# Cached keys of the sample branch: 32x32 blocks turned by VectorE, scores as four row-tiled products

## The chip, the core and the metric

The kernel runs on one core of a Trainium2 chip. The metric is the device time of one execution in microseconds; the lower, the better. The kernel before takes 2191.76 us (median of three runs, 2189.55 to 2191.92).

A core has a matrix engine (TensorE, PE in the profile, with its weight loads shown apart as PEld), VectorE (DVE), ScalarE (ACT), GpSimd (POOL) and SyncE (SP), which here issues nearly all transfers. [...] Matrix products write to PSUM, of which there are eight banks of 128 partitions and 512 float32 columns.

## The reference

One inference step of one layer: a prompt of 256 tokens and 8 sample sequences of 8 new tokens each, that have 1024 cached tokens. All rows go through one input projection; two mixers (a gated delta rule and an attention over chosen keys) run on its columns, and the results are merged and projected again. The change concerns the second mixer for the sample sequences:

```python
def indexer_topk(qi, wi, kidx, q_pos, topk):
    logits = jnp.einsum('bqhd,bkd->bqhk', qi, kidx) * (IDX_DH ** -0.5)
    score = jnp.einsum('bqhk,bqh->bqk', jax.nn.relu(logits), wi) * (IDX_HEADS ** -0.5)
    score = jnp.where(causal[None], score, -jnp.inf)
    _, idx = lax.top_k(score, topk)
    return idx, idx <= q_pos[None, :, None]

def sparse_attention(q, k_sel, v_sel, valid):
    s = jnp.einsum('bqngd,bqknd->bqngk', qg, k_sel) * (ATT_DH ** -0.5)
    s = jnp.where(valid[:, :, None, None, :], s, -jnp.inf)
    p = jax.nn.softmax(s, axis=-1)
    return jnp.einsum('bqngk,bqknd->bqngd', p, v_sel)

# dsa_sample: kidx, k and v of the 1024 past tokens come from paged caches
# through page_table; the 8 new tokens of the sequence stand behind them
```

For each sample sequence the indexer has 16 heads x 8 tokens = 128 query rows of length 128 against 1024 cached index keys, and the attention has 16 heads in two groups with one key head each (n = 0, 1), so 2 x 64 query rows of length 128 against 2 x 1024 cached keys. 256 keys are kept per token.

## The kernel before, in words

**Main stream.** `stream` walks through 464 units. A unit is half of the 2048 rows of a 128-column block of a weight matrix. Its float32 weights are loaded (`raw`, six halves of 512 KB), split by ScalarE into a rounded high part (`whi`) and by VectorE into the rest (`wlo`), and 24 products with the 320 activation columns are made (`pm<-xh,whi`, `pm<-xl,whi`, `pm<-xh,wlo`). `split_ahead` splits two units ahead, with three buffers of each part. Units 0 to 119 are the attention columns and gates, unit 120 opens the delta-rule part.

**Side work.** Everything else is written as Python generators. `side_round` is called twice a unit, after 12 of the 24 products and at the end, and lets each generator emit its next piece if the planner's own clock (`Clock`) says that its operands are there. The order on every engine is so fixed when the program is built; the clock's costs only decide where a piece falls between the main products. All engines run that order; the real waits are semaphores.

**The sample branch** (`sample_branch`, L1337 and on) is one generator over the 8 sequences b, first for the indexer, then for the attention.

- A gather by GpSimd brings keys into a buffer of the `a8` ring (`a` in the profile): partition p holds 8 rows of the cache, each of 128 (indexer) or 2 x 128 numbers (attention).
- `tr4` turns a 128x128 piece by four TensorE transposes of 32 partitions each (`ps<-ident,a`, 32x32 results over four PSUM banks), and `out4` brings the four banks back by two ScalarE and two VectorE copies. An indexer sequence takes 8 pieces (32 transposes), an attention sequence 16 (64 transposes). The probabilities `pr` of the attention are turned in the same way; the change leaves that as it is.
- Indexer (L1369 to L1401): `ps<-a,qiS`, two products of 128x512 with the query as weights, and `ps<-kidxT,qiS` for new keys, float32 (two instructions to a product); ReLU by ScalarE; a product with head weights (`wsel`); the row goes to `scs` by a transfer.
- `scs` [64, 1088] goes through 32 rounds of `max` and `match_replace` on VectorE, and gives the mask `bs`.
- Attention (from L1440): for three column ranges the mask is laid into PSUM by a bf16 product (`ps<-bs,esel`), and the scores are added (`ps<-a,qS`, 64 output partitions for each n, and `ps<-kT,qS` for the new keys). Then a maximum, exponentials with sums, the turned probabilities, the product with V (`ps<-a,a`), and `sample_out`.

**Buffers.** Six PSUM banks (`ps`) serve all side work, two (`pm`) the main stream. Transfers are issued by SP in program order; an instruction at the head of its queue that waits holds those behind it.

## Time and profile before

| | before |
|---|---|
| median of 3 runs | 2191.76 us |
| the profiled execution | 2190.04 us |
| its span in the profile | 2188.3 us |
| busy: PE / PEld / DVE / ACT / POOL | 99% / 93% / 63% / 46% / 21% |
| granted TensorE clock | 0.998 |
| mean transfer rate | 198 GB/s |

In the profile a row of the timeline has the start, the duration, engine, line, operation, the names (out<-in, buffer numbers left out), shapes, type and a count. Matrix products are pipelined: a product's duration holds its way through the array, and the next one starts before it has ended, so costs are read from start to start. All instructions go through one helper and carry line 61; the tile names tell them apart.

### The profile page before, as it was taken

The page shows a single profiled execution, that of the slowest core. Times are in us where ns is not written, and L with a number is a line of the kernel's source. Part 1 is how long each engine was busy: PE and PEld are TensorE (multiplying, and loading weights), DVE is VectorE, ACT ScalarE, POOL GpSimd, SP SyncE. Part 2 cuts the span into 40 slices and gives each one's busy share as a digit, 9 for nine tenths or more (in the row PEclk, how much of TensorE's full clock was granted, in tenths as well). Part 3 has the DMA queues.
Part 4 walks back from the last instruction along what each step waited for, and adds up shares of the span by engine and source line. Part 5 has one row for each costly group of instructions (what it writes and reads, how often), then busy time and mean ns, then how long its engine had stood idle before and what let it go on. Part 6 is the DMA issues. An engine that isn't in the chain of part 4 may idle for free.

```text
span 2188.3 us, 43683 instructions
## 1 busy us (share of the span) xinstructions
PE 2157.9 (99%) x17151; PEld 2041.2 (93%) x17151; DVE 1384.4 (63%) x2807; ACT 1002.9 (46%) x2207; POOL 458.2 (21%) x624
## 2 busy tenths in 40 slices
PE   7999999999999999999999999999999999999997
PEld 6889988999888999899999999999999999999997
DVE  4665447789644477777777777777756545545543
ACT  3225464343343455474646464646445434233343
POOL 1000100000000008361717171717270000000000
PEclk9999999999999999999999999999999999999999
DMA  9985549765666667686768686867786966655562
GB/s 333 354 281 151 155 120 264 218 188 142 186 209 203 192 170 196 169 217 186 217 177 219 178 220 177 219 178 212 184 233 187 279 194 201 177 151 155 154 183 87
DMA packets 709839, 433.14 MB, mean 198 GB/s; under 512 B 67936, under 2 KB 697024, under 8 KB 707328
## 3 DMA queue, kind: packets, MB, share of 16 engines
q1 hardware_dynamic: 705536, 407.67, 66.1%
q0 software_dynamic: 3616, 21.02, 2.8%
q8 instruction: 135, 2.21, 0.4%
q10 hardware_dynamic: 480, 1.65, 0.2%
q14 instruction: 72, 0.59, 0.1%
HBM read 382.09 MB, written 47.89 MB: 196 GB/s over the span
## 4 chain that ended last, share of the span: by engine, by line
PE 67%; issue 23%; DVE 5%; DMA 3%; ACT 1%; SPq 0%; DVEq 0%; POOL 0%; POOLq 0%
PE pm L61 51%; PE ps L61 17%; DVE S L61 2%; DMA raw<-in_w_ada_dram 1%; DVE ps L61 1%; ACT ot L61 1%; DVE wlo L61 1%; DVE w L61 0%; DMA raw<-in_w_in_dram 0%; DMA cst<-in_conv_w_dram 0%; ACT vt L61 0%; SPq L61 0%; ACT whi L61 0%; DVE sc L61 0%; DMA c<-in_c_sample_dram 0%
## 5 line engine op out<-in xcount | busy, mean ns | idle before, releaser
L61 PE MATMUL pm<-xh,whi 128*128 128x320 f32 x3284 | 1004.4, 319 | 2.0 <-ACT whi L61 1.7
L61 PE MATMUL pm<-xl,whi 128*128 128x320 f32 x3284 | 971.6, 309 | 0.3 <-DVE xl L61 0.3
L61 DVE TENSOR_TENSOR wlo<-raw,whi 128x1024 fp32r<-128x1024 f32 x474 | 596.4, 1265 | 311.1 <-ACT whi L61 294.4
L61 PEld LDWEIGHTS pm<-xh,whi 128*128 128x128 f32 x3284 | 617.3, 188 | 34.3 <-issue 25.5
L61 PEld LDWEIGHTS pm<-xl,whi 128*128 128x128 f32 x3284 | 617.5, 188 | 1.5 <-DVE xl L61 0.8
L61 ACT ACTIVATE whi<-raw 128x1024 fp32r<-128x1024 f32 x474 | 497.9, 1058 | 158.7 <-PE pm L61 141.4
L61 PE MATMUL pm<-xh,wlo 128*128 128x320 f32 x3284 | 553.4, 309 | 0.0
L61 PEld LDWEIGHTS pm<-xh,wlo 128*128 128x128 f32 x3284 | 499.4, 188 | 0.0
L61 POOL TENSOR_TENSOR X<-X,tmpx 48x31 f32<-48x31 f32 (+15 forms) x248 | 184.0, 742 | 19.4
L61 POOL TENSOR_TENSOR tmpx<-blk,X 48x31 f32<-48x31 f32 (+15 forms) x248 | 156.4, 631 | 53.1 <-DMA blk<-d_b 21.7
L61 PE MATMUL pm<-y1h,whi 128*128 128x320 f32 x512 | 151.3, 309 | 1.1 <-ACT y1h L61 1.1
L61 PE MATMUL pm<-y1l,whi 128*128 128x320 f32 x512 | 151.2, 308 | 0.1
L61 DVE SCALAR_TENSOR_TENSOR ps<-xp,cs,ps 128x344 f32<-128x344 f32 x192 | 111.5, 581 | 6.8
L61 POOL TENSOR_TENSOR sc<-sc,mh 128x6 f32<-128x6 f32 (+1 forms) x24 | 43.6, 1815 | 328.6 <-DVE ct L61 136.6
L61 POOL TENSOR_TENSOR rfin<-rfin,mh 128x3 f32<-128x3 f32 x1 | 0.8, 848 | 486.7 <-DVE rfin L61 486.7
L61 PEld LDWEIGHTS pm<-y1h,whi 128*128 128x128 f32 x512 | 95.9, 187 | 1.3 <-ACT y1h L61 1.3
L61 PEld LDWEIGHTS pm<-y1l,whi 128*128 128x128 f32 x512 | 96.0, 187 | 0.3 <-DVE y1l L61 0.3
L61 PE MATMUL pm<-y1h,wlo 128*128 128x320 f32 x512 | 85.4, 308 | 0.0
L61 PEld LDWEIGHTS pm<-y1h,wlo 128*128 128x128 f32 x512 | 77.8, 187 | 0.0
L61 DVE SCALAR_TENSOR_TENSOR S<-S,gtr,ps 128x128 f32<-128x128 f32 x256 | 67.5, 344 | 0.1
L61 ACT ACTIVATE a<-ps 128x256 f32<-128x256 f32 (+3 forms) x96 | 50.1, 557 | 37.8 <-PE ps L61 36.6
L61 ACT ACTIVATE xp<-pm 128x256 f32<-128x256 f32 (+1 forms) x128 | 32.0, 303 | 69.7 <-PE pm L61 69.7
(360 smaller groups left out, 2317.5 us busy)
## 6 DMA issues: line engine op xcount, KB each, us to landing
raw<-in_w_in_dram SPq DMA_DIRECT2D x336, 512.0 KB
raw<-in_w_pa_dram SPq DMA_DIRECT2D x64, 512.0 KB
rawx<-in_w_ada_dram SPq DMA_DIRECT2D x18, 1024.0 KB
a<-in_w_ada_dram SPq DMA_DIRECT2D x16, 1024.0 KB
S<-in_state_gdn_dram SPq DMA_DIRECT2D x32, 512.0 KB
out_dram<-S SPq DMA_DIRECT2D x32, 512.0 KB
raw<-in_w_pb_dram SPq DMA_DIRECT2D x32, 512.0 KB
raw<-in_w_out_dram SPq DMA_DIRECT2D x32, 512.0 KB
```

The costliest lines, as they stand in the source:

```text
L61: made = fn(*args, **kw)
```

## The change

The stationary operand of the scores becomes a piece of the query that covers 32 of its 128 numbers, and the moving operand the 32 partitions of a block-turned key buffer.

1. `turn` replaces `tr4` and `out4` for keys: one VectorE transpose of 128x1024 in 32x32 blocks (per indexer sequence), two in place (per attention sequence). A turned block has the numbers of one 32-group j in its partitions, and there are four groups g of cache rows on the four partition groups.
2. The query must lie in all four partition groups. `spread` writes `qiS` (or `qS`) to a DRAM tensor in four transfers, in the layout [b, 32, 4, 128]; `fill` reads the piece of one sequence back four times, once per partition group, into half of the query's own buffer (`slot`, two sequences at a time). The next sequence but one is filled after the products of the present one.
3. The scores of an indexer sequence are 16 products (j, g) of 32 partitions, 128 weights and 256 columns, that add up over j in four banks (one per g). Those of an attention sequence are 32 products (j, g, n) of 32 partitions, 64 weights and 256 columns.
4. The new keys' scores are made for all sequences at once in `spread` (`newi`, `newk`) by products of 8 columns; VectorE adds `newk` later.
5. The mask is laid into five banks in place of three, with all 128 partitions as the contraction (`esel`, `bs` padded with zeros). There are five maxima and five exponentials in place of three each, four ReLU pieces in place of three; the orders of columns in `rl`, `sb`, `bs` and `pr` follow.
6. `Clock.cost` gets a factor for the new products.

```diff
-            part *= 0.62 if k <= 64 else 1.0
+            part *= 0.29 if k == 32 and rhs.shape[1] == NB else 0.62 if k <= 64 else 1.0
...
+        self.d_qi, self.d_q = (self.dram.tile([NB, 32, 4, 128], F32, name=n) for n in ("d_qi", "d_q"))
...
         if self.bq_n == 16:
-            self.flags.add("qS")
+            self.spawn(self.spread(self.qS, self.d_q, self.newk, [self.kT[:, n, :] for n in range(2)], 2, "qR"))
...
+    def fill(self, q, dram, b):
+        t = self.slot(q, b)
+        for j in range(4):
+            self.nc.sync.dma_start(t[32 * j:32 * j + 32], dram[b])
+
+    def spread(self, q, dram, new, keys, heads, flag, **kw):
+        yield self.ready(q, *keys)
+        yield from self.need(self.ps_side)
+        p = self.psum()
+        w = 128 // heads
+        for b in range(NB):
+            for n in range(heads):
+                s = slice(w * n, w * n + w)
+                self.mm(p[s, 8 * b:8 * b + 8], q[:, b, s], keys[n][:, NP + 8 * b:NP + 8 * b + 8], skip=True)
+        self.act(new, p[:, 0:64].rearrange("p (b t) -> p b t", t=TS), **kw)
+        self.ps_side.put(p)
+        for j in range(4):
+            self.nc.sync.dma_start(dram[:, :, j, :].rearrange("b r h -> r b h"), q[32 * j:32 * j + 32])
+        yield max(self.idle(q), self.ready(dram))
+        self.fill(q, dram, 0)
+        self.fill(q, dram, 1)
+        self.flags.add(flag)
...
-            for c0, c1 in self.SEGS:
-                yield from self.need(self.ps_side)
-                p = self.psum()
-                rhs = raws[b][:, 1024 + c0:1024 + c1] if c0 < NKEY else self.kidxT[:, NP:NT]
-                self.mm(p[:, 0:c1 - c0], self.qiS[:, b, :], rhs)
-                self.act(rl[:, c0:c1], p[:, 0:c1 - c0], AF.Relu, scale=SC)
-                self.ps_side.put(p)
+            yield from self.need(self.ps_side, 4)
+            ps = [self.psum() for _ in range(4)]
+            kt = raws[b][:, 1024:2048].rearrange("p (e j c) -> p j e c", e=8, j=4)
+            q = self.slot(self.qiS, b)
+            for j in range(4):
+                for g in range(4):
+                    r = slice(32 * g, 32 * g + 32)
+                    self.mm(ps[g][:, 0:256].rearrange("p (e c) -> p e c", e=8), q[r, j, :], kt[r, j],
+                            start=(j == 0), stop=(j == 3), skip=True)
...
+            if b + 2 < NB:
+                self.fill(self.qiS, self.d_qi, b + 2)
             if b + 1 < NB:
-                yield from keys_t(b + 1)
+                turn(raws[b + 1][:, 1024:2048], raws[b + 1][:, 0:1024])
...
-            for j in range(16):
-                self.tr4(ps, j, K[b][:, 128 * j:128 * j + 128])
-            self.out4(ps, 16, K[b])
+            for c in range(0, 2048, 1024):
+                turn(K[b][:, c:c + 1024], K[b][:, c:c + 1024])
...
+            for g, (p, w) in enumerate(zip(ps, width)):
+                self.mm(p[:, 0:w], es, self.bs[:, 256 * g:256 * g + w], start=True, stop=True)
+            for j in range(4):
+                for g in range(4):
+                    for n in range(2):
+                        r, s = slice(32 * g, 32 * g + 32), slice(64 * n, 64 * n + 64)
+                        self.mm(ps[g][s, 0:256].rearrange("r (e c) -> r e c", e=8), qr[r, j, s], ktv[r, n, j],
+                                start=False, stop=True, skip=True)
+            own = ps[4][:, 8 * b:8 * b + 8]
+            self.tt(own, own, self.newk[:, b, :], OP.add)
```

The order on TensorE in the indexer, at the second sequence, before; `pm` rows are the main stream, `a_1756` the keys of this sequence and `a_1757` those of the next.

```order
L61 MATMUL pm_65<-xl,whi_80 128x320
L61 MATMUL ps_68<-a_1756,qiS 128x512
L61 MATMUL ps_67<-a_1756,qiS 128x512
L61 MATMUL ps_70<-kidxT,qiS 128x64
...
L61 MATMUL pm_65<-xh,wlo_83 128x320 x8
L61 MATMUL ps_71<-ident,a_1757 128x32
...
L61 MATMUL ps_67<-a_1758,wsel 8x512 x2
L61 MATMUL ps_67<-a_1758,wsel 8x64
```

Three score products stand in one place, and half a unit later 32 transposes (of which one is shown) stand ahead of the product with the head weights. The same place after the change, with `a_1760` as the keys:

```order
L61 MATMUL pm_66<-xl,whi_79 128x320
L61 MATMUL ps_69<-a_1760,qiS 128x256
L61 MATMUL ps_67<-a_1760,qiS 128x256
L61 MATMUL ps_70<-a_1760,qiS 128x256
L61 MATMUL ps_71<-a_1760,qiS 128x256
...
L61 MATMUL pm_66<-xh,wlo_82 128x320 x8
L61 MATMUL ps_72<-a_1762,wsel 8x512 x2
L61 MATMUL ps_72<-newi,wsel 8x8
```

The four products stand there four times over (j = 0 to 3), the transposes are gone from TensorE, and 12 main products still stand between the scores and `wsel`.

The order on TensorE at the scores of the first attention sequence, before:

```order
L61 LDWEIGHTS esel
L61 MATMUL ps_67<-bs,esel 128x512
L61 MATMUL ps_67<-a_1755,qS 64x512 x2
L61 LDWEIGHTS esel
L61 MATMUL ps_71<-bs,esel 128x512
L61 MATMUL ps_71<-a_1755,qS 64x512 x2
L61 LDWEIGHTS esel
L61 MATMUL ps_69<-bs,esel 128x64
L61 MATMUL ps_69<-kT,qS 64x64 x2
```

Mask and scores alternate. After the change:

```order
L61 MATMUL ps_67<-bs,esel 128x256
L61 LDWEIGHTS esel
L61 MATMUL ps_69<-bs,esel 128x64
L61 MATMUL ps_71<-a_1759,qS 64x256 x2
L61 MATMUL ps_70<-a_1759,qS 64x256 x2
L61 MATMUL ps_72<-a_1759,qS 64x256 x2
L61 MATMUL ps_67<-a_1759,qS 64x256 x2
```

Five masks now come first (the last two are shown), then all products of the keys, eight for each j. The next use of the probabilities on TensorE (their transposes) stands 48 main products and the 64 key transposes later before, and 36 main products later after the change.

The order on VectorE behind the scores of the second attention sequence after the change:

```order
L61 TENSOR_TENSOR ps_67<-ps_67,newk 128x8
L61 TENSOR_REDUCE st_1766<-ps_67 128x1
L61 TENSOR_REDUCE st_1766<-ps_68 128x1
L61 TENSOR_REDUCE st_1766<-ps_71 128x1
L61 TENSOR_REDUCE st_1766<-ps_70 128x1
L61 TENSOR_REDUCE st_1766<-ps_72 128x1
L61 TENSOR_REDUCE st_1766<-st_1766 128x1 x2
L61 RECIPROCAL st_1766<-st_1766 128x1
L61 STREAM_TRANSPOSE a_1760<-a_1760 128x1024 x2
L61 TENSOR_TENSOR wlo_82<-raw_77,whi_79 128x1024
```

The two transposes of the next sequence's keys stand between the reciprocal and the next low part `wlo` of the main stream.

The order on SP in the middle of the indexer after the change:

```order
L61 DMA qiS<-d_qi 32x512 x4
L61 DMA scs<-a_1763 8x1088
L61 DMA raw_76<-in_w_in_dram 128x8x128 x2
L61 DMA qiS<-d_qi 32x512 x4
L61 DMA scs<-a_1763 8x1088
L61 DMA raw_77<-in_w_in_dram 128x8x128 x2
```

Before, a sequence had two loads `raw` and one `scs` there; four short reads of the query come to them.

## The prediction

> **What bounds the kernel now.** I read the page first, for the engines' shares, then the table of stretches for the two stages of the sample branch, and then the timeline of TensorE inside them. Timeline columns are start, duration, engine, line, operation, names, shape, count.

> ```profile
> span 2188.3 us, 43683 instructions
> PE 2157.9 (99%) x17151; PEld 2041.2 (93%) x17151; DVE 1384.4 (63%) x2807; ACT 1002.9 (46%) x2207; POOL 458.2 (21%) x624
> PE 67%; issue 23%; DVE 5%; DMA 3%; ACT 1%; SPq 0%; DVEq 0%; POOL 0%; POOLq 0%
> ```

> PE is busy nearly always, and the chain of waits that ended last (third row) runs mostly over PE. The stretches:

> ```profile
> 224.00:333.00 109.00, 109.00 (x892) 92.45 (x892) 46.84 (x94) 62.41 (x109) 7.47 (x8) 1.00 0.50 138
> 333.00:570.00 237.00, 237.00 (x1818) 226.20 (x1817) 195.13 (x318) 91.39 (x194) 3.98 (x7) 1.00 0.70 202
> 570.00:750.00 180.00, 180.00 (x1988) 152.95 (x1987) 81.24 (x146) 69.22 (x140) 15.30 (x26) 1.00 0.62 188
> ```

> The columns of the stretches are window, length, then busy PE, PEld, DVE, ACT, POOL, the granted clock, DMA share and GB/s. The indexer lies in the first stretch, the 32 selection rounds in the second, the attention in the third. PE is busy all the time in each, at clock 1.00, so it never waits there. A busy PE is not proof of a full one, so I go by start times: they show that the main products follow each other at a fixed rate, and that each piece of side work pushes all later ones back.

> ```profile
> 233.17 7.04 PE pm L61 x48
> ```

> This is 0.147 us a main product. The cost of a side piece is the start of the second main product behind it, less the start of the last one ahead of it, less 2 x 0.147 = 0.29. What the change takes from PE in these stages is time of the kernel; what it moves to VectorE or SP costs nothing until PE has to wait.

> **The indexer.** Before, a sequence costs PE these pieces:

> ```profile
> 262.51 0.31 PE L61 MATMUL pm<-xl,whi 128*128 128x320 f32 x1
> 262.66 1.88 PE L61 MATMUL ps<-a,qiS 128*128 128x512 f32 x4
> 264.37 0.33 PE L61 MATMUL ps<-kidxT,qiS 128*128 128x64 f32 x2
> 264.51 0.39 PE L61 MATMUL pm<-xh,whi 128*128 128x320 f32 x1
> 264.74 0.31 PE L61 MATMUL pm<-xl,whi 128*128 128x320 f32 x1
> ...
> 266.44 0.69 PE L61 MATMUL ps<-ident,a 32*128 32x32 f32 x32
> 267.06 1.03 PE L61 MATMUL ps<-a,wsel 128*8 128x512 f32 x6
> ```

> Scores: 264.74 - 262.51 - 0.29 = 1.94 us. Transposes: 267.06 - 266.44 = 0.62 us. The new scores are 16 float32 products of 32 partitions by 256 columns, so 32 instructions. The delta-rule part already has that form:

> ```profile
> 1014.09 1.15 PE L61 MATMUL ps<-w,ktok 32*128 32x256 f32 x16
> 1015.17 0.41 PE L61 MATMUL pm<-xh,whi 128*128 128x320 f32 x1
> ...
> 357.04 0.27 PE L61 MATMUL ps<-bp,ident_b 128*128 128x256 bf16 x1
> 357.15 0.60 PE L61 MATMUL ps<-kT,q 128*128 128x256 f32 x2
> 357.58 0.51 PE L61 MATMUL ps<-sel,s 128*128 128x9 f32 x4
> ```

> On the full array one instruction of 256 columns takes (357.58 - 357.15) / 2 = 0.215 us. Sixteen of 32 partitions take 1.08 us, not 3.44: four run side by side, 4 x 0.215 = 0.86, and 0.22 goes to the change of form. So the new scores take 8 x 0.215 + 0.22 = 1.94, and 0.20 for entering and for the slowed first main product (the attention's transposes below: 1.32 - 1.12). That is 2.14, 0.20 more than before, 1.6 us for eight sequences. The transposes give back 8 x 0.62 = 5.0.

> The new keys' product in `spread` has 16 instructions of 8 columns with 128 weights:

> ```profile
> 370.20 0.51 PE L61 MATMUL ps<-sel,s 128*128 128x9 f32 x4
> 370.57 0.22 PE L61 MATMUL ps<-bp,ident_b 128*128 128x128 bf16 x1
> ```

> Four such take 0.37 us, so 16 take 1.5; below, at the rate of the attention's transposes (0.0175 each), 0.3. I take 1.5, the nearer form. Indexer: 1.6 - 5.0 + 1.5 = -1.9 us.

> **The attention.** Before:

> ```profile
> 570.14 0.31 PE L61 MATMUL pm<-xl,whi 128*128 128x320 f32 x1
> 570.38 1.20 PE L61 MATMUL ps<-ident,a 32*128 32x32 f32 x64
> 571.50 0.41 PE L61 MATMUL pm<-xh,whi 128*128 128x320 f32 x1
> 571.75 0.31 PE L61 MATMUL pm<-xl,whi 128*128 128x320 f32 x1
> ...
> 574.97 0.31 PE L61 MATMUL pm<-xl,whi 128*128 128x320 f32 x1
> 575.21 0.39 PE L61 MATMUL ps<-bs,esel 64*128 64x512 bf16 x1
> 575.53 1.08 PE L61 MATMUL ps<-a,qS 128*64 128x512 f32 x4
> 576.54 0.39 PE L61 MATMUL ps<-bs,esel 64*128 64x512 bf16 x1
> ...
> 578.00 0.34 PE L61 MATMUL ps<-kT,qS 128*64 128x64 f32 x4
> 578.26 0.41 PE L61 MATMUL pm<-xh,whi 128*128 128x320 f32 x1
> 578.51 0.31 PE L61 MATMUL pm<-xl,whi 128*128 128x320 f32 x1
> ```

> Transposes: 571.75 - 570.14 - 0.29 = 1.32 us, of which 1.12 are the 64 themselves. Eight times some 1.3 gives back 10.4. Scores with mask: 578.51 - 574.97 - 0.29 = 3.25. After it there are four masks of 256 columns (357.15 - 357.04 = 0.11 each) and one of 64 (0.05 at the most): 0.49. Then 64 instructions of 32 partitions, 64 weights, 256 columns. Two halves n run side by side already: four instructions of 512 columns take 576.54 - 575.53 = 1.01, not 4 x 0.43. If both divisions hold at once, eight run side by side: 8 rounds x 0.215 + 0.22 = 1.94. With 0.20 as above the piece costs 2.63, 0.62 less, and eight give back 5.0. `spread` for the attention has 32 instructions with 64 weights; four of the `kT,qS` form took 0.26, so 2.1 us, between 0.6 (transposes' rate) and 3.0 (`sel` rate). Attention: -10.4 - 5.0 + 2.1 = -13.3 us.

> **What moves to other engines.** VectorE gets 24 transposes of 128x1024, which no row shows. The nearest are these, of the same size:

> ```profile
> L61 DVE TENSOR_TENSOR wlo<-raw,whi 128x1024 fp32r<-128x1024 f32 x108 | 131.6, 1220 | 107.6 <-ACT whi L61 107.6
> L61 DVE TENSOR_REDUCE st<-ps 128x1 f32<-128x256 f32 x16 | 6.6, 411 | 0.0
> ```

> ```profile
> 580.87 0.16 DVE L61 TENSOR_REDUCE st<-st 128x1 f32<-128x3 f32 x1 [1.87 <-ACT a L61]
> ```

> The first two rows are groups (busy, mean ns of one, idle before), the third shows the wait for the exponentials. I take 1.2 us; the bounds are half of it and, for two passes, 2.4. That is 10 us in the first stretch and 20 in the third, where VectorE is idle for 62 and 99. What hides them is the lead of the splits. Behind a score VectorE does 0.2 + 5 maxima (4 x 0.41 + 0.2) + 0.2, waits for five exponentials (three took 1.87; I take 2.5), then 0.3, then two transposes 2.4, then the next `wlo` 1.2: 8.6 us. That low part belongs to the third unit ahead. PE first passes 12 + 24 + 24 + 16 = 76 main products, 11.1 us, so 2.5 us are spare. ScalarE gets two exponentials more, SP 72 transfers.

> ```profile
> SPq L61 <- ACT a L61: 43.8, 8, 6.7
> ```

> SP has been held by the `scs` row for up to 6.7 us with weight loads behind it, eight times, and PE did not wait; a `fill` held until a product ends stays below that. The first fill hangs on a round trip through DRAM, with 60 main products (8.8 us) between `spread` and the first score; that and small waits for ReLU or exponentials I put at 1 us in all (between 0 and 4).

> **Sum.** -1.9 - 13.3 + 1.0 = -14.2 us against the profiled execution's 2190.04: 2175.8. The median of the runs stands 1.7 above that execution, so **2177 us**. Behind unit 130 the order on PE is the same as before, and PE bounds that part too, so the gain should reach the end.

> **Rivals.**
> (a) *The attention's eight tiles run only four at a time.* The case for it: in no row are partition and column divisions used together on long products. Against: each alone is perfect. Then 16 rounds, 1.72 us more a sequence, +13.8: 2191, no change. [...] The `a,qS` row, two column halves on all rows in 1.01 us, speaks against it.
> (b) *The probabilities come late.* The longer chain (2.1 maxima + 0.2 + 2.5 exponentials = 4.8) must end in 36 main products, 5.3 us, where it had 8.6 before. One split `whi` of ScalarE (1.06 us by the page) in between makes PE wait 0.6 a sequence: +5, 2182.

> ```profile
> L61 ACT ACTIVATE whi<-raw 128x1024 fp32r<-128x1024 f32 x474 | 497.9, 1058 | 158.7 <-PE pm L61 141.4
> ```

> (c) *Slower: VectorE's transposes hold the splits.* From 2.4 us a transpose on the spare 2.5 us are gone, and PE waits twice the excess in each of seven sequences. At 3.4 the gain is eaten; at four passes of 1.22 (4.9 us) it is 2 x 2.5 x 7 = 35 us: 2212. Nothing in the profile shows more than one pass. [...]

> **Chances.** The forecast 0.70, with an own range of 2172 to 2181 from the bounds of the two `spread` products and of the small waits; (b) 0.10; (a) 0.12; (c) 0.05; 0.03 for a lost round trip or another wait. Reaching from the forecast over (b) towards (a), the range is 2170 to 2188. About 0.2%, 4.4 us, can be told from no change: faster has the forecast and (b), 0.80; same has (a), 0.12; slower 0.08.

> **What would show it.** In the profile after: `a,qiS` pieces of some 1.94 us with 32 instructions, `a,qS` of the same length with 64 (3.7 would be (a)), 256 instructions left in `ident,a`; PE without idle between 224 and 750; `STREAM_TRANSPOSE` near 1.2 us (above 2.4 with waits of PE for `wlo` would be (c)); waits of PE for `a` ahead of the probabilities' transposes would be (b). The forecast is wrong if the gain up to unit 120 is not found in the starts, or if PE waits at unit 120, where the store of `ybuf` now begins 1.5 units later.

## The result, and the profile after

| | before | after |
|---|---|---|
| median | 2191.52 us (6 runs, 2189.55 to 2191.92) | 2173.64 us (6 runs, 2172.43 to 2176.31) |
| the profiled execution | 2190.04 us | 2176.31 us |
| its span | 2188.3 us | 2174.6 us |

The ratio is 0.9922, with a 95% interval of 0.9909 to 0.9934: 17.9 us less by the medians. The forecast was a median of 2177 us, a gain of 14.2.

The page after; the rows answer to those of before.

```profile
span 2174.6 us, 43708 instructions
PE 2144.6 (99%) x17071; PEld 2045.5 (94%) x17071; DVE 1395.1 (64%) x2823; ACT 995.3 (46%) x2217; POOL 462.2 (21%) x627
PE 68%; issue 23%; DVE 5%; ACT 2%; DMA 2%; SPq 0%; DVEq 0%; POOL 0%; POOLq 0%; ACTq 0%
```

PE lost 13.3 us of busy time and VectorE gained 10.7. The stretches, the third cut at 740, where this kernel's attention ends (window, length, busy PE, PEld, DVE, ACT, POOL, granted clock, DMA share, GB/s):

```profile
224.00:333.00 109.00, 109.00 (x864) 97.79 (x862) 56.32 (x105) 56.57 (x113) 8.20 (x10) 1.00 0.57 158
333.00:570.00 237.00, 237.00 (x1847) 224.31 (x1847) 189.43 (x297) 92.77 (x184) 3.37 (x5) 1.00 0.71 208
570.00:740.00 170.00, 170.00 (x1947) 157.14 (x1946) 91.04 (x174) 69.03 (x160) 15.24 (x26) 1.00 0.72 213
```

PE still has no idle time in them, at clock 1.00. (The windows are fixed in time, and the end of the indexer now lies behind 333, so the busy times don't compare piece by piece; the balance below does.) Now the new pieces in the timeline of TensorE, in the order new keys and scores of the indexer, new keys and scores of the attention:

```profile
251.90 0.31 PE L61 MATMUL pm<-xl,whi 128*128 128x320 f32 x1
252.05 1.85 PE L61 MATMUL ps<-kidxT,qiS 128*128 128x8 f32 x16
253.75 0.39 PE L61 MATMUL pm<-xh,whi 128*128 128x320 f32 x1
253.98 0.31 PE L61 MATMUL pm<-xl,whi 128*128 128x320 f32 x1
...
271.05 0.31 PE L61 MATMUL pm<-xl,whi 128*128 128x320 f32 x1
271.29 2.01 PE L61 MATMUL ps<-a,qiS 32*128 32x256 f32 x32
273.23 0.41 PE L61 MATMUL pm<-xh,whi 128*128 128x320 f32 x1
273.48 0.31 PE L61 MATMUL pm<-xl,whi 128*128 128x320 f32 x1
...
433.06 0.31 PE L61 MATMUL pm<-xl,whi 128*128 128x320 f32 x1
433.30 1.11 PE L61 MATMUL ps<-kT,qS 128*64 128x8 f32 x32
434.34 0.41 PE L61 MATMUL pm<-xh,whi 128*128 128x320 f32 x1
434.59 0.31 PE L61 MATMUL pm<-xl,whi 128*128 128x320 f32 x1
...
575.77 0.64 PE L61 MATMUL ps<-bs,esel 128*128 128x256 bf16 x5
576.34 1.98 PE L61 MATMUL ps<-a,qS 32*64 32x256 f32 x64
578.26 0.42 PE L61 MATMUL pm<-xh,whi 128*128 128x320 f32 x1
578.51 0.31 PE L61 MATMUL pm<-xl,whi 128*128 128x320 f32 x1
```

By the prediction's rule (second main product behind, less the last one ahead, less 0.29) these cost 1.79, 2.14, 1.24 and, over all eight sequences, 2.59 us. The key transposes are gone from PE. Applied to every side piece of the sample branch, the rule gives this balance, in us for the whole kernel:

| term | forecast | in the trace |
|---|---|---|
| indexer: scores | +1.6 | 8 x (2.134 - 1.940) = +1.6 |
| indexer: key transposes | -5.0 | -5.1 |
| indexer: new keys | +1.5 | +1.8 |
| attention: key transposes | -10.4 | -10.3 |
| attention: scores and mask | -5.0 | 8 x (2.592 - 3.249) = -5.3 |
| attention: new keys | +2.1 | +1.2 |
| small waits | +1.0 | 0 |
| sum | -14.2 | -16.1 |

With all other side work counted in as well, the pieces between unit 17 and unit 128 fell from 147.64 to 131.67 us, 16.0 less, and those between unit 0 and unit 17 by 0.8: together 16.8. From the start of unit 0 to that of unit 130 the changed kernel is 16.75 us faster, so the pieces account for all of it. At the first main product of unit 192, in the timeline of before and then of after, it is 16.5 us ahead:

```profile
1069.06 0.35 PE L61 MATMUL ps<-ident,cst 92*128 92x92 f32 x2 [0.46 <-DMA cst<-in_conv_w_dram]
1069.20 0.39 PE L61 MATMUL pm<-xh,whi 128*128 128x320 f32 x1
```

```profile
1052.71 0.39 PE L61 MATMUL pm<-xh,whi 128*128 128x320 f32 x1
```

Two small things stand in this number that are no pieces of the sample branch: unit 0 began 0.95 us later in this execution, and at unit 192 the kernel before waited 0.46 us for a transfer (first row), which makes 0.65 of the lead: 16.75 - 0.95 + 0.65 = 16.45.

At the end of this execution only 13.7 us of the lead were left. The other 2.8 went in one place, behind the delta-rule part; a row of its timeline and two of its stretches:

```profile
1708.95 0.42 PE L61 MATMUL pm<-y1h,whi 128*128 128x320 f32 x1 [1.94 <-ACT y1h L61]
```

```profile
1706.00:1710.00 4.00, 1.95 (x9) 1.20 (x8) 1.15 (x4) 1.59 (x4) 0.00 (x0) 0.98 0.70 208
1710.00:1714.00 4.00, 4.00 (x19) 4.00 (x18) 4.00 (x5) 2.55 (x4) 0.00 (x0) 0.60 0.75 216
```

PE waited 1.94 us for `y1h` (1.06 before), and then the granted clock was 0.60 for four microseconds. The profiled execution is the slowest of its six, 2.7 us over their median, and that of before is 1.5 under its own; that is why the medians lie 17.9 apart and the two profiles only 13.7.

### The profile page after: what moved, and what is told of

Read it like the earlier page. It is cut to its first block, busy times and chain, and to the rows that moved or that the text cites. A ratio compares the mean times of both kernels' runs of the same rounds, so it can differ in the third digit from the quotient of the medians.

```text
span 2174.6 us, 43708 instructions
## 1 busy us (share of the span) xinstructions
PE 2144.6 (99%) x17071; PEld 2045.5 (94%) x17071; DVE 1395.1 (64%) x2823; ACT 995.3 (46%) x2217; POOL 462.2 (21%) x627
## 4 chain that ended last, share of the span: by engine, by line
PE 68%; issue 23%; DVE 5%; ACT 2%; DMA 2%; SPq 0%; DVEq 0%; POOL 0%; POOLq 0%; ACTq 0%
PE pm L61 52%; PE ps L61 16%; DVE S L61 2%; DMA raw<-in_w_ada_dram 1%; DVE ps L61 1%; ACT ot L61 1%; DVE wlo L61 1%; DVE w L61 0%; ACT whi L61 0%; ACT vt L61 0%; DMA c<-in_c_sample_dram 0%; SPq L61 0%; DVE vt L61 0%; DVE sc L61 0%; DVE sga L61 0%
## 5 line engine op out<-in xcount | busy, mean ns | idle before, releaser
L61 PE MATMUL pm<-xh,whi 128*128 128x320 f32 x3284 | 1004.1, 319 | 2.0 <-ACT whi L61 1.7
L61 PE MATMUL pm<-xl,whi 128*128 128x320 f32 x3284 | 971.6, 309 | 0.3 <-DVE xl L61 0.3
L61 DVE TENSOR_TENSOR wlo<-raw,whi 128x1024 fp32r<-128x1024 f32 x474 | 593.1, 1259 | 291.0 <-ACT whi L61 275.6
L61 PEld LDWEIGHTS pm<-xh,whi 128*128 128x128 f32 x3284 | 616.8, 188 | 39.6 <-issue 31.2
L61 PEld LDWEIGHTS pm<-xl,whi 128*128 128x128 f32 x3284 | 617.5, 188 | 1.6 <-DVE xl L61 0.8
L61 ACT ACTIVATE whi<-raw 128x1024 fp32r<-128x1024 f32 x474 | 498.9, 1059 | 169.1 <-PE pm L61 151.0
L61 PE MATMUL pm<-xh,wlo 128*128 128x320 f32 x3284 | 553.3, 309 | 0.0
L61 PEld LDWEIGHTS pm<-xh,wlo 128*128 128x128 f32 x3284 | 499.5, 188 | 0.0
L61 POOL TENSOR_TENSOR X<-X,tmpx 48x31 f32<-48x31 f32 (+15 forms) x248 | 180.6, 728 | 19.5
L61 POOL TENSOR_TENSOR tmpx<-blk,X 48x31 f32<-48x31 f32 (+15 forms) x248 | 160.4, 647 | 55.1 <-DMA blk<-d_b 23.4
L61 PE MATMUL pm<-y1h,whi 128*128 128x320 f32 x512 | 151.8, 310 | 1.9 <-ACT y1h L61 1.9
L61 PE MATMUL pm<-y1l,whi 128*128 128x320 f32 x512 | 151.9, 310 | 0.1
L61 DVE SCALAR_TENSOR_TENSOR ps<-xp,cs,ps 128x344 f32<-128x344 f32 x192 | 111.5, 581 | 6.8
L61 POOL TENSOR_TENSOR sc<-sc,mh 128x6 f32<-128x6 f32 (+1 forms) x24 | 44.7, 1864 | 324.9 <-DVE ct L61 165.4
L61 POOL TENSOR_TENSOR rfin<-rfin,mh 128x3 f32<-128x3 f32 x1 | 0.8, 848 | 489.4 <-DVE rfin L61 489.4
L61 PEld LDWEIGHTS pm<-y1h,whi 128*128 128x128 f32 x512 | 96.6, 189 | 2.2 <-ACT y1h L61 2.2
L61 PEld LDWEIGHTS pm<-y1l,whi 128*128 128x128 f32 x512 | 96.6, 189 | 0.7 <-DVE y1l L61 0.6
L61 PE MATMUL pm<-y1h,wlo 128*128 128x320 f32 x512 | 86.4, 311 | 0.0
L61 PEld LDWEIGHTS pm<-y1h,wlo 128*128 128x128 f32 x512 | 78.5, 190 | 0.0
L61 DVE SCALAR_TENSOR_TENSOR S<-S,gtr,ps 128x128 f32<-128x128 f32 x256 | 67.4, 341 | 0.1
L61 ACT ACTIVATE ot<-ot,sc 128x128 f32<-128x128 f32 x96 | 29.9, 390 | 74.2 <-DVE sc L61 74.2
L61 ACT ACTIVATE xp<-pm 128x256 f32<-128x256 f32 (+1 forms) x128 | 32.0, 304 | 67.6 <-PE pm L61 67.6
```

Source lines behind the costliest of these rows:

```text
L61: made = fn(*args, **kw)
```

## The experiments

Theory 1 is the prediction's: the gain is the PE time of the sample branch's side pieces, and the work that went to VectorE, SP and DRAM is free. Its rivals differ from run to run. Each kernel is the changed one with the edit shown (`...` stands for lines left out); the ratio compares it with the kernel before on the same chip. Three chips were used, and the kernel before takes 2191.01, 2190.13 and 2190.93 us on them. The changed kernel was run again on the first of them only, so where a kernel of the second or third is set against it, two differences are given: that of the medians, and that of the gains over the kernel before.

### The changed kernel again

No edit.

> The changed kernel itself, for a second profile and as the measure for the other runs. Theory 1 (the gain is the PE time of the side pieces of the sample branch and nothing else): about 2173.6 us; main products behind unit 128 start 16.5 us earlier than before, and so they do at the end. In the first profile the lead fell from 16.5 to 13.7 us between 1709 and 1714 us, where PE waited 1.9 us for y1h and the granted clock then was 0.60. By theory 1 this is chance and isn't there again, or is there in the kernel before as often; the rival, that the change brings it, has it again at the same place.

Measured: 2174.09 us (2172.91 to 2175.18), ratio 0.9919 (0.9903 to 0.9936). The lead over the first profile of before was 17.2 us at unit 192 and 14.8 at the end. The wait for `y1h` was there again, 1.8 us, and so was the slow clock behind it. The loss thus belongs to the place, and more than one execution has it. Over the twelve profiled executions of this study (all kernels), the two starts around this wait lie 1.1 to 2.4 us apart (1.4 in the one profile of before), and the slow clock came in three of the twelve: this one, the first profile and the kernel with three transposes below. It came at 1.81, 2.11 and 2.35 us and not at 1.88 and 1.97, so the length of the wait doesn't decide alone, and what does is not shown. Why `y1h` is later in some executions, and whether the change has a part in it, stays open: there is one profile of before, and kernels with the change lie on both sides of it (1.1 with the head weights on four column groups).

### Four neighbours on different parts of the array, not eight

```diff
-            for j in range(4):
-                for g in range(4):
-                    for n in range(2):
+            for n in range(2):
+                for j in range(4):
+                    for g in range(4):
```

> The attention's scores with the loop over the two halves n outermost: the same 64 instructions, but eight neighbours no longer lie on eight different parts of the array, only on four. Theory 1 (eight ran side by side in the changed kernel): 16 rounds of 0.215 us in place of 8, so the piece of scores and mask rises from 2.59 to 4.31 us, +1.72 x 8 = +13.8, about 2187 us. Rival (the array takes four at a time whatever the order, and the time of the piece comes from somewhere else): the piece stays at 2.59 us and the time at 2174.

Measured: 2180.72 us (2179.87 to 2182.24), ratio 0.995 (0.9934 to 0.9967), 6.6 us more than the changed kernel. The piece rose to 3.505 us, +0.91, half of what theory 1 said; 8 x 0.91 = 7.3. (A part of the array is here 32 of its rows by 64 of its columns; there are four groups of rows, g, times two halves, n.) First the scores' row of the changed kernel (second profile), then of this one:

```profile
575.19 1.98 PE L61 MATMUL ps<-a,qS 32*64 32x256 f32 x64
```

```profile
575.39 2.90 PE L61 MATMUL ps<-a,qS 32*64 32x256 f32 x64
```

The starts of the 64 single records tell why both expectations missed. Times in us, a wave being the instructions that start within 0.05 us of each other:

```
changed kernel, 8 to a wave: 575.19 575.46 575.67 575.89 576.11 576.32 576.54 576.75
n outermost, 4 to a wave
  first stream:              575.39 575.65 575.87 576.09 576.30 576.52 576.73 576.95
  second stream:             576.33 576.59 576.81 577.03 577.24 577.46 577.67 577.89
```

In the changed kernel eight instructions run at once, in eight waves 0.216 us apart: rival (a) of the prediction is out. With n outermost there are two streams of eight waves of four. A part takes one instruction per 0.216 us, so they must be the two halves; the last wave, at 577.89, carries the semaphore updates, as the last products of the second half should. The second stream begins with the first one's fifth wave, not behind its eighth. So the second half had begun while three waves of the first were still to start. Theory 2, the author's reading of these starts: a part of the array takes four instructions, one at work and three waiting, and only then does PE stop at the next one for it.

### Eight instructions in succession on one part

```diff
-            for j in range(4):
-                for g in range(4):
-                    for n in range(2):
+            for g in range(4):
+                for n in range(2):
+                    for j in range(4):
```

> The attention's scores with the loop over the four 32-groups j innermost: eight instructions in succession for the same part of the array. Theory 2 (formed on the run with n outermost: a part of the array takes up to four instructions, one in work and three waiting, and PE passes on to the next part only then): 7 x 4 + 8 = 36 rounds of 0.216 us, the piece takes 7.8 + 0.9 = 8.7 us. Rival (PE passes on as long as anything is ahead, the order doesn't matter): below 4 us. Second rival (nothing waits ahead, one in work only): 7 x 7 + 8 = 57 rounds, 13 us.

Measured, in one run: 2268.57 us; the piece 11.7 to 13.1 us. By its length alone the piece would speak for the second rival, 13 us, as much as for theory 2, 8.7. The starts of single records tell them apart; behind them stand the piece in the timeline of this kernel, then two of its stretches:

```
first instruction on a part:   578.03 578.95 579.87 580.79 581.71 582.63
```

```profile
578.03 11.68 PE L61 MATMUL ps<-a,qS 32*64 32x256 f32 x64
```

```profile
578.00:582.60 4.60, 4.60 (x38) 3.39 (x37) 1.06 (x4) 0.09 (x1) 0.00 (x0) 1.00 0.52 158
582.60:590.00 7.40, 7.40 (x31) 4.31 (x29) 1.10 (x3) 0.00 (x0) 0.02 (x1) 0.51 0.08 20
```

Each part starts 0.92 us behind the one ahead of it, which is four instructions of 0.216 and a little, as theory 2 has it; seven would be 1.5. From 582.6 the granted clock is 0.51, the intervals are 0.427 in place of 0.216, and the piece gets longer by that. So the starts agree with theory 2, and its price of 8.7 failed on the clock. The theory rests on the starts of two profiles, one of each order, and this kernel ran only once.

### Three VectorE transposes in place of one

```diff
             for c in range(0, 2048, 1024):
                 turn(K[b][:, c:c + 1024], K[b][:, c:c + 1024])
+                for _ in range(2):
+                    (the same transpose again)
```

> Each of the attention's two VectorE transposes per sequence is done three times in place, which gives the same keys; 4 transposes of 1.18 to 1.22 us more a sequence, VectorE +38 us in all, order on PE unchanged. Theory 1 with the prediction's price (spare of VectorE 2.5 us a sequence, beyond it PE waits twice the excess): 3.6 us for each of the two, 2 x 1.2 x 7 = +17, about 2190 us, with waits of PE for wlo. Rival (the lead of the splits is longer than the prediction counted, VectorE catches up before PE comes): under +3 us, no waits of PE for wlo between 570 and 740 us.

Measured: 2183.68 us (2182.76 to 2184.94), ratio 0.9967 (0.9955 to 0.9978), +9.6. In between: PE does wait, but less than priced. PE's waits from 565 to 745 us (total, times, longest):

```profile
PE pm L61 <- DVE wlo L61: 4.2, 7, 0.9
PE ps L61 <- DVE a L1463: 2.6, 1, 2.6
```

The second row is the first sequence alone, whose keys came late; the first is the seven others. The main products fall back by 0.8 us a sequence, for four more transposes of

```profile
L1463 DVE STREAM_TRANSPOSE a<-a 128x1024 f32<-128x1024 f32 x32 | 39.9, 1246 | 1.1
```

that is 5.0 us. If PE loses just what exceeds the spare, the spare is some 4.2 us, not the 2.5 of the prediction; this is an estimate from these rows.

### The same for one of the two

```diff
             for c in range(0, 2048, 1024):
                 turn(K[b][:, c:c + 1024], K[b][:, c:c + 1024])
+                for _ in range(2 if c else 0):
+                    (the same transpose again)
```

> One of the attention's two VectorE transposes per sequence is done three times, the other once: 2.4 to 2.5 us more of VectorE a sequence, order on PE unchanged. The run with both done three times put +4.9 us a sequence on VectorE and made PE wait 0.8 to 0.9 us for wlo, so by theory 1 the spare is near 4 us, and this costs nothing but up to 0.5 us ahead of the first sequence: 2174 to 2174.5 us, no waits of PE for wlo. Rival (VectorE's time in this stage is time of the kernel in proportion): half of that run's +9.6, 2179 us.

Measured: 2173.67 us (2172.39 to 2175.29), ratio 0.9918 (0.9901 to 0.9934). No wait of PE is listed between 150 and 760 us, and only the first score piece is longer, by 0.13 us. VectorE's time isn't time of the kernel until the spare is used up: 2.5 us more cost nothing after the first sequence, 5.0 cost 0.8 us in each.

### The key transposes back on PE, as pieces of their own

```diff
+        self.junk = a.tile([128, 4], F32, name="junk")
...
                 k_trans(b + 1)
+                yield from self.need(self.ps_side, 4)
+                ps = [self.psum() for _ in range(4)]
+                for j in range(16):
+                    self.tr4(ps, j, self.ident)
+                for g, p in enumerate(ps):
+                    self.act(self.junk[:, g:g + 1], p[:, 0:1])
+                    self.ps_side.put(p)
```

> The 64 TensorE transposes of 32 partitions per attention sequence are put back, in seven of the eight sequences, but on a constant and with four one-column copies in place of the evacuation, beside the VectorE transposes that stay. Nothing else of the change is undone. Theory 1 (the key transposes were worth their PE time, 1.3 us a sequence): +7 x 1.35 = +9.4, about 2183 us. Rival (much of the gain came with the evacuations and the PSUM banks that the key transposes held): +5 us or less.

Measured: 2189.49 us (2188.78 to 2192.51), ratio 0.9994 (0.9984 to 1.0003): +15.4, more than either expectation. The pieces cost 1.315 us each, 9.2 for seven, as theory 1 has it. The rest is elsewhere. Two stretches of this kernel, and its timeline behind 745 us:

```profile
570.00:742.00 172.00, 172.00 (x2228) 159.67 (x2227) 88.89 (x158) 66.65 (x172) 12.69 (x19) 1.00 0.71 213
742.00:764.00 22.00, 17.57 (x219) 14.92 (x212) 7.03 (x23) 6.18 (x20) 4.09 (x8) 0.77 0.28 89
```

```profile
746.91 1.98 PE L61 MATMUL ps<-a,qS 32*64 32x256 f32 x64
748.82 0.33 PE L61 MATMUL ps<-ident,a 128*128 128x128 f32 x1
752.83 1.42 PE L61 MATMUL ps<-ident,a 32*128 32x32 f32 x33 [3.68 <-ACT a L61]
754.48 4.02 PE L61 MATMUL ps<-a,a 128*64 128x128 f32 x32 [0.23 <-ACT a L61]
```

The new pieces delayed every sequence in the planner's order. When unit 120 came, the last one wasn't done, and unit 120 can't begin without it. So its scores, exponentials and products ran one behind the other with no main product in between: PE waited 4.4 us for `a`, and the clock was 0.77. In the second half of unit 119 the starts were only 1.4 us behind the changed kernel's, in the second half of unit 120 they were 18.9 behind. The run changed two things, and its total says nothing about the transposes alone.

### The same transposes, the order untouched

```diff
+            for k in range(16):
+                for g in range(4):
+                    r = slice(32 * g, 32 * g + 32)
+                    (transpose of the constant, ident[r], into ps[g], ahead of the probabilities' own)
             for k in range(8):
                 self.tr4(ps, k, prf[:, 128 * k:128 * k + 128])
```

> The previous run put the attention's TensorE transposes back as pieces of their own, and that moved the side work: up to unit 119 it was only 1.4 us behind, and then the last attention sequence had nothing beside it at unit 120. Here the 64 transposes (on a constant, into the banks and in the piece of the probabilities' transposes, in all eight sequences) leave the order on every other engine as it is in the changed kernel. Theory 1 (the gain is PE time): +8 x 64 x 0.0175 = +9.0, about 2183 us, PE without waits between 570 and 740. Rival (the transposes cost more than their PE time, as the +15.4 of the previous run could be read): above +12.

Measured: 2181.73 us (2180.27 to 2183.8), ratio 0.9961 (0.9946 to 0.9976): +7.6 on the changed kernel by the medians, +8.5 by the gains over the kernel before. The two rows of this piece:

```profile
583.70 1.19 PE L1522 MATMUL ps<-ident 32*128 32x32 f32 x64
584.71 0.90 PE L61 MATMUL ps<-ident,a 32*128 32x32 f32 x33
```

The 64 take 584.71 - 583.70 = 1.01 us, the piece rose from 0.854 to 1.849, and 8 x 0.995 = 8.0. The main products fell back by 0.99 us eight times and by nothing else up to unit 125, and PE didn't wait there. Theory 1 holds, with 0.0155 us a transpose in place of 0.0175.

### The attention's part alone

The indexer's lines are those of the kernel before.

> The change in the attention alone; the indexer is that of the kernel before. Theory 1 by the pieces measured in the changed kernel: the indexer's part of the gain is 8 x (2.134 - 1.940) + 1.79 - 5.1 = -1.8, so this kernel takes 1.8 us more than the changed one, about 2175.7 us. Rival (the indexer's change also loosens the selection behind it, which waits for its last row): 3 us or more above the changed kernel.

Measured: 2175.77 us (2174.62 to 2176.69), ratio 0.9933 (0.9919 to 0.9946): 1.7 us more than the changed kernel by the medians, 2.6 by the gains over the kernel before. It agrees with theory 1, but at intervals of 0.13% it would agree with the rival's 3 us as well; what carries the point are the pieces, 1.940 us for scores and 1.778 for transposes with head weights, as before.

### A step further: head weights on four column groups

```diff
-            segs = (rl[:, 0:512], rl[:, 512:1024], self.newi[:, b, :])
-            for q, v in enumerate(segs):
-                self.mm(p[32 * q:32 * q + 8, 0:v.shape[1]], self.wsel[:, b, :], v, skip=True)
+            for q in range(4):
+                self.mm(p[32 * q:32 * q + 8, 0:256], self.wsel[:, b, :], rl[:, 256 * q:256 * q + 256], skip=True)
+            self.mm(p[0:8, 256:264], self.wsel[:, b, :], self.newi[:, b, :], skip=True)
```

> A step beyond the changed kernel: in the indexer the product with the head weights has eight output rows; its two 512-column products on two groups of 32 output columns become four of 256 columns on four groups. Theory 1 (side pieces on PE are time of the kernel, and products on different parts of the array run side by side): the piece falls from 1.16 to about 0.73 us (two rounds of 0.216 less), -0.43 x 8 = -3.4 against the changed kernel, about 2170.5 us. Rival (four column groups that read the same 128 rows don't run together): the piece stays at 1.16 us or above, no gain.

Measured: 2170.72 us (2169.38 to 2173.86), ratio 0.9912 (0.9899 to 0.9926). The product in the changed kernel, then here:

```profile
266.61 0.60 PE L61 MATMUL ps<-a,wsel 128*8 128x512 f32 x2
266.62 0.20 PE L61 MATMUL ps<-newi,wsel 128*8 128x8 f32 x2
267.04 0.60 PE L61 MATMUL ps<-a,wsel 128*8 128x512 f32 x2
267.57 0.41 PE L61 MATMUL pm<-xh,whi 128*128 128x320 f32 x1
```

```profile
266.55 0.62 PE L61 MATMUL ps<-a,wsel 128*8 128x256 f32 x8
266.98 0.20 PE L61 MATMUL ps<-newi,wsel 128*8 128x8 f32 x2
267.11 0.42 PE L61 MATMUL pm<-xh,whi 128*128 128x320 f32 x1
```

The piece is 0.76 us, 0.40 less, so four column groups on the same 128 rows do run side by side, and 8 x 0.40 = 3.2. The median is 3.4 below that of the changed kernel, by the gains over the kernel before it is 2.5; the intervals of the two ratios overlap, and again the pieces carry the point.

### And the mask in the form of the scores

```diff
...
-            for g, (p, w) in enumerate(zip(ps, width)):
-                self.mm(p[:, 0:w], es, self.bs[:, 256 * g:256 * g + w], start=True, stop=True)
+            for g, w, c in ((0, 64, 256), (0, 256, 0), (1, 256, 0), (2, 256, 0), (3, 256, 0)):
+                for n in range(2):
+                    r, s = slice(32 * g, 32 * g + 32), slice(64 * n, 64 * n + 64)
+                    self.mm(ps[4 if c else g][s, 0:w], es[r, s], self.bs[r, b // 4, c:c + w], skip=True)
```

> On top of the head weights' product on four column groups (piece 0.76 us): the attention's mask goes in by products in the form of the scores, 32 rows and 64 output columns, eight at a time, in place of five on the full array; for that the mask lies in four groups of 32 rows, ten small VectorE operations in place of two. And the new keys' product of the indexer is made in 64-column halves as that of the attention. Theory 1: mask 4 x 0.11 + 0.05 and a change of form of 0.12 (last mask product to the first score) become one wave of 0.11 and a short one, the piece falls from 2.59 to about 2.12 us, -0.47 x 8 = -3.8; new keys 1.79 to 1.23, -0.6; with the -3.1 of the run before about 2166.5 us. Rival (the later mask moves the attention towards its end at unit 120): no better than 2170.7, with waits of PE behind unit 120.

Measured: 2169.32 us (2168.03 to 2170.64), ratio 0.9902 (0.9885 to 0.9918). The piece in this kernel (the new keys' product and the mask's new layout are left out of the diff):

```profile
590.37 0.31 PE L61 MATMUL pm<-xl,whi 128*128 128x320 f32 x1
590.61 0.33 PE L61 MATMUL ps<-bs,esel 32*64 32x64 bf16 x10
590.75 1.91 PE L61 MATMUL ps<-a,qS 32*64 32x256 f32 x64
592.59 0.41 PE L61 MATMUL pm<-xh,whi 128*128 128x320 f32 x1
592.84 0.31 PE L61 MATMUL pm<-xl,whi 128*128 128x320 f32 x1
```

From the first mask product to the first score it is 0.14 us, where it was 576.34 - 575.77 = 0.57. The piece is 2.18 us, 0.41 less, and the new keys' product 1.23: 8 x 0.41 + 0.55 = 3.8. PE has no wait behind unit 120 that the changed kernel hasn't. Within the two profiled executions the starts are 3.9 us earlier than the run before's at unit 192 (each counted from the start of its main stream) and 3.1 at the end. By the medians only 1.4 are seen (2.2 by the gains over the kernel before), and the two ratios' intervals overlap; that this step gains is shown by the pieces, not by the times. Its median is the lowest of all, and both steps together are 2174.09 - 2169.32 = 4.8 us below the changed kernel.

## Why the prediction was right, point by point

**What bounds.** Right. The side pieces up to unit 128 take 16.8 us less, and, counted from unit 0, PE reaches unit 130 16.75 us sooner; the transposes put back into PE's queue came back as time, 8.0 us of piece and 7.6 to 8.5 us of median. What went to VectorE is free: 28.8 us of transposes, and 20 more in the run with one of two done three times. That the median came out 3.4 us under the forecast is for the larger part due to the two terms named below (1.9 us). The rest is no larger than what single executions differ by in the start of unit 0 (0.95), a wait for a transfer (0.65) and the loss at `y1h` (2.8), and is not settled further.

**Eight at a time.** Right: 64 instructions in eight waves of eight, 0.216 us apart. Nor did the weight loads hold the products apart, although the two halves n share a row group: by the single records of the changed kernel's first profile, the weight loads of the second wave start between 576.397 and 576.444 us, while the eight products begun between 576.344 and 576.390, of 0.425 us each, are in flight on all four row groups. The form of the scores, the 0.22 for the change of form and the 0.20 for entering gave 2.14 and 2.63; the trace has 2.134 and 2.592.

**Where a size was off.** The new keys' product of the attention: 2.1 forecast, 1.2 measured. It was priced by the `kT,qS` form of the kernel before, four instructions of 64 columns in 0.26 us; with 8 columns an instruction takes 0.033 ((434.34 - 433.30) / 32). That is nearer to the lower bound, the rate of the 32x32 transposes (0.0175). The indexer's took 1.79 for 1.5. The small waits, put at 1.0, were none: the first score found its query, and no ReLU, exponential or `fill` held PE up. These two terms, 0.9 and 1.0, are what the forecast gave away; the other rows of the balance were off by 0.3 or less, up and down, and cancel.

**VectorE's transposes.** 1.2 us taken, 1.224 measured, in the group of all 24:

```profile
L61 DVE STREAM_TRANSPOSE a<-a 128x1024 f32<-128x1024 f32 x24 | 28.8, 1224 | 0.0
```

Rival (c)'s mechanism is real, as the threefold run shows, but its spare was too small: PE lost 0.8 us a sequence where the prediction's price gave 2.4, and a spare of some 4.2 us in place of 2.5 would account for it. Which link of the chain of VectorE was counted too early is not settled.

**Rival (b), late probabilities.** Not seen: PE waits for nothing between 224 and 740 us. The wait for the five exponentials is 2.29 us where 2.5 was estimated, in the timeline of VectorE after:

```profile
582.24 0.16 DVE L61 TENSOR_REDUCE st<-st 128x1 f32<-128x5 f32 x1 [2.29 <-ACT a L61]
```

The wait does happen where the cover is gone, in the run with the transposes as pieces of their own: 3.68 us at once.

**SP and the round trip.** SP's waits for side products rose by little, from 36.1 us in 25 times, and those for `a` fell from 43.8 us (total, times, longest, after):

```profile
SPq L61 <- PE ps L61: 44.3, 36, 4.8
SPq L61 <- ACT a L61: 8.4, 3, 3.7
```

In the attention SP now also stands for `ybuf`, 66.1 us in 10 times where it was 9.9 in 3, with weight loads at the head of its queue. No product came late by any of it: PE waits for nothing between 224 and 740 us.

**To the end.** The order behind unit 130 is the same, and the lead arrives but for the loss at `y1h`, which the prediction didn't foresee: it took that part as bounded by PE throughout. The point to watch, unit 120, was the right one for another reason than the one given: in the run that stumbled there it was not the store of `ybuf`, but that the last sequence has to be through.

## What to carry to other kernels

Where TensorE is always busy, cost a change by the side pieces from start to start and leave out the engines it moves work to; then test that cover by doubling the moved work until something waits (here 20 us more on VectorE cost nothing in the times, 40 cost 9.6). Small products gained here by running side by side on parts of the array that had stood empty: the scores with their mask went from 3.25 to 2.59 us a sequence and with the tiled mask to 2.18, the product with the head weights, eight output rows, from 1.16 to 0.76 on four column groups. Keep neighbours in the queue on different parts of the array: with the halves n outermost the piece took 0.91 us more, with j innermost it took at least 11.7, a part of it at half clock. An experiment that adds a piece also moves the planner's order; put it inside a piece that is there, or its total may speak of a deadline and not of the piece.

## What the runs showed of the hardware

**A change of form.** Between the start of the last mask product on the full array, of only 64 columns, and that of the first score 0.12 us pass, where a whole 256-column mask product takes 0.11. With the tiled mask the first score starts 0.09 us behind the last mask product, of 256 columns; the change now lies ahead of the mask, 590.61 - 590.37 = 0.24 us behind a main product in place of 0.15. So it is moved and not saved, and what the tiled mask gains is mainly that the masks run side by side. A pause of some 0.1 us is what the traces show of a change of form; whether the array is empty then they don't show.

**The clock.** It fell to half without PE being idle in the run with j innermost: PE was busy for all 4.60 us from 578.00 to 582.60, at clock 1.00, with the scores going to one part of the array after the other, and the clock was 0.51 from there to 590.00. And it fell in three executions behind the wait for `y1h`, of 1.5, 1.8 and 1.9 us there, for 3.4 us (main products 0.27 us apart in place of 0.147). Behind a wait of 1.66 us with j innermost they stayed 0.147 apart, and behind one of 1.6 in the run with one of two transposes done three times the clock was 1.00. The clock records of the changed kernel's first trace give 1696.42 us at full, 3.413 at half and 450.56 at full, those of the trace of before 2167.46 at full; the long ones are close to 497, 132 and 635 times the 3.413 of the short one. No run set the clock on purpose: neither what makes it fall nor what sets these lengths is shown.
